# Where the operands of a split-fp32 decoder trunk start in on-chip memory: multiples of 512 bytes

## The chip, the cores and the metric

One core of a Trainium2 chip runs the whole kernel. The metric is the device time of one execution in microseconds (us). Several runs of the unchanged kernel gave a median of 1013.87 us, from 1013.25 to 1014.61.

## The reference

A two-layer causal decoder trunk on 512 tokens of width 1024, all in float32. Layer 0 mixes the tokens by a convolution module and latent attention side by side, layer 1 by causal pooling over windows of 2 to 16 tokens. After each of them stands a gated MLP with a short causal convolution on the gate branch.

```python
def conv_ffn(h, w_up, ffn_conv_w, ffn_conv_b, w_down):
    uv = h @ w_up                                  # 1024 -> 2 * 2816
    u, v = uv[..., :D_FF], uv[..., D_FF:]
    u = causal_dwconv(u, ffn_conv_w, ffn_conv_b)   # 3 taps
    return (jax.nn.silu(u) * v) @ w_down           # 2816 -> 1024

for l in range(DEPTH):                             # DEPTH = 2
    if l % 2 == 0:
        x = x + conv_mla_mixer(rmsnorm(x, norm_mix_e[e]), ...)
    else:
        x = x + pool_mixer(rmsnorm(x, norm_mix_o[o]), ...)
    x = x + conv_ffn(rmsnorm(x, norm_ffn[l]), w_up[l], ...)
return rmsnorm(x, final_norm)
```

## The kernel before

The activations lie transposed, with channels on the 128 partitions and the 512 tokens along the free dimension, so a tile of activations is 128 x 512 floats, 2048 bytes in each partition.

**Split operands.** A float32 matrix product is made of three matmuls in the type fp32r. Each operand is split into a high half (`act.copy` to fp32r, on ScalarE) and a low half (the rest, `dve.tensor_tensor` with subtract, on VectorE); `split` (L96) and `split_scaled` (L101) do that. `mm3` (L107) issues high x high (L108), high x low (L109) and low x high (L110) into one PSUM bank. Its second argument is the stationary operand (loaded into the array by a LDWEIGHTS), its third the moving one (streamed through). In nearly all stages the weights are stationary and the activations moving: 128 x 128 of weights, 512 bytes in each partition, against 128 x 512 of activations. The names in the profile follow this: `ps<-xgh,hi` is a matmul into a PSUM bank `ps` which streams the high half of an activation (`xgh`) against the high half of a weight tile (`hi`).

**Kept and streamed.** Weights are streamed: `fetch` (L147) issues a DMA of up to 128 x 1024 floats into one of three `raw` buffers, and `prepare` (L153) splits it into one of three `hi` and three `lo` buffers. All nine come from the pool "weights". One such tile serves eight stationary operands (`part`, L124), 512 bytes apart. Activations are kept: `xg` (the normed input of a stage, eight tiles and two halves, names `xgh` and `xgl`, in pools "xg0" to "xg2" on the right side of memory), `s4` (latents, attention output and convolution output, in the pool "mixer" on the left side; the profile calls them `s`), and the gate tiles (`gh` and `gl`, 22 of each, in the pool "gate", which takes the place of "mixer" later).

**Stages, in order of time.** A start in which the input and the first weights arrive and the first projection runs (to about 38 us); the other projections (to 98); keys, values and attention with convolution taps in between (to 168); the output projection (to 235); the up projection of layer 0 (22 tiles of `u` and `v`, each 24 matmuls of `mm3`'s kind) and its down projection (to 605); the pooling mixer (to 627), which first projects with the weights as moving operand (256 columns) and then multiplies by banded matrices that lie in gate tiles (L869, L870, L872); the up and the down projection of layer 1 (from 657), whose last tile runs in two halves of 256 columns (`last_down`, L751); the output. The value projection inside the attention stage (L576 to L583) swaps the roles, too: `s4` is stationary and the weights are moving, with 512 columns.

**What sets the order.** The order in which the program is written sets each engine's order; a pool's buffers set what waits for what. Neither depends on addresses.

**Where tiles start.** The pools are laid out one after the other: "consts", "resid", "weights", "temps", "small" and "mixer"/"gate" upward from the left; a pool "pad" with one tile of `PAD` floats and then "xg" downward from the right. So the size of any tile shifts all that lies behind it. Two tiles exist only to shift others: `w_pad` (L144, 128 floats ahead of `raw`) and the tile of p_pad (L273, `PAD` = 184 floats).

Of the kernel before, what the change touches and what calls it, by code (L numbers as in the profile page):

```python
# [8 lines left out]
F32 = mybir.dt.float32  # L9
# [6 lines left out]
P = 128  # L16
S = 512
# [5 lines left out]
CW = 31  # L23
# [14 lines left out]

WARM = 40
PE_TAPS = 16  # L40
PAD = 184
GLU, LAT, BLK, END = 3, 4, 2, 0


# [1 line left out]
def kernel(  # L46
# [24 lines left out]
    p_w = ctx.enter_context(tc.tile_pool(name="weights", bufs=3))  # L71
    p_t = ctx.enter_context(tc.tile_pool(name="temps", bufs=8))
# [6 lines left out]
    def uid(s):  # L79
        count[0] += 1  # L80
        return f"{s}{count[0]}"
# [7 lines left out]
    def temp():  # L89
        return p_t.tile([P, 2 + S], F32, tag="t", name=uid("t"))[:, :S]  # L90
# [25 lines left out]

    def halves(pl, tag, n, bufs):


        hl = [[pl.tile([P, S], F32R, tag=tag + i, bufs=bufs, name=uid(tag + i)) for _ in range(n)]  # L120
              for i in "hl"]
        return list(zip(*hl))
# [18 lines left out]
        stream += [(w_up[2 * NF * l + i], 1024) for i in range(2 * NF)]  # L141
        stream += [(w_down[NF * l + i], 1024) for i in range(NF)]
    raws, ready = [], []
    p_w.tile([P, P], F32, tag="pad", bufs=1, name="w_pad")  # L144
    given = [0]

    def fetch():  # L147
# [25 lines left out]

    idle = p_c.tile([P, P], mybir.dt.bfloat16, name="idle")
    dve.memset(idle, 0.0)
    misc = p_s.tile([P, 24], F32, tag="misc", bufs=1, name="misc")
    spare, floor, q_scale = misc[:, 0:1], misc[:, 4:8], misc[:, 8:12]
    mv = misc[:, 12:20].rearrange("p (a b) -> p a b", b=2)
# [91 lines left out]


    p_pad = tc.alloc_tile_pool(name="pad", bufs=1, side="right")
    p_pad.tile([P, PAD], F32, name="pad")  # L273
    p_m = tc.alloc_tile_pool(name="mixer", bufs=1, side="left", reuse_waits="tile")
    p_xg = tc.alloc_tile_pool(name="xg0", bufs=KD, side="right", reuse_waits="tile")

    def xg_tiles(pl):
        return halves(pl, "xg", KD, KD)
# [94 lines left out]
    u, ys, work, pe_work = [], [], [], []  # L373

    def conv(m):
        cw = C_CW + CW * m
        side = p_m.tile([P, S], F32, tag="side", bufs=4, name=uid("side"))
        ys.append(side)
        st = {}

        def open_acc():
            st["acc"] = aux("conv")
            act.activation(  # L383
                st["acc"], u[m][:, CW - 1 : CW - 1 + S], AF.Identity,
                bias=c(C_CB + m), scale=c(cw + CW - 1),
            )

        def pe_tap(j):
            if j == 0:
                st["acc"] = aux()  # L390
            d = p_m.tile([P, P], F32, tag="tapped", bufs=4, name=uid("tap"))
            pool.tensor_scalar(d, ident, c(cw + j), None, op0=ALU.mult)
            pe.matmul(st["acc"], d, u[m][:, j : j + S], start=j == 0, stop=j == PE_TAPS - 1)  # L393

        def tap(j):
            while m == 3 and pe_work:
                pe_work.pop(0)()
            if not st:
                open_acc()
            i = dve.scalar_tensor_tensor(  # L400
                st["acc"], u[m][:, j : j + S], c(cw + j), st["acc"],
                op0=ALU.mult, op1=ALU.add,
            )
            if held:
                tc.add_manual_dep(
                    i.ins, held.pop().ins.name,
                    mybir.DependencyInfo(
                        mybir.DependencyClass.NoSync, mybir.DependencyReason.DATA
                    ),
                    reason="background",  # L410
                )

        def close():
            bias = c(C_CB + m) if m == 3 else 0.0
            act.activation(side, st["acc"], AF.Identity, bias=bias, scale=1.0)

        n_pe = PE_TAPS if m == 3 else 0
        pe_work.extend((lambda j=j: pe_tap(j)) for j in range(n_pe))
        work.extend((lambda j=j: tap(j)) for j in range(n_pe, CW if m == 3 else CW - 1))
        work.append(close)  # L420
# [8 lines left out]
    def glu(ps_a, ps_g):  # L429
        t = temp()  # L430
        dve.tensor_tensor(t, ps_g, rows0, op=ALU.mult)
        s = temp()
        act.activation(s, t, AF.Sigmoid)
        if len(u) == 3:
            act.activation(spare, s[:, 0:1], AF.Exp)
        dve.tensor_tensor(s, s, rows0, op=ALU.mult)
        ut = p_m.tile([P, CW - 1 + S], F32, tag="u", bufs=4, name=uid("u"))
        pool.memset(ut[:, : CW - 1], 0.0)
        dve.tensor_tensor(ut[:, CW - 1 :], ps_a, s, op=ALU.mult)
        u.append(ut)  # L440
        conv(len(u) - 1)

    def s4():
        return p_m.tile([P, 2, S], F32R, tag="s4", bufs=8, name=uid("s4"))

    glu(acc4[0], acc4[1])
    glu(acc4[2], acc4[3])
    def latent(n, gain, width):
        parts, stat = [], Squares(width, dve)
# [18 lines left out]
    for _ in range(2):  # L468
        ps_a = project()
        pump(GLU)  # L470
        ps_g = project()
        glu(ps_a, ps_g)
        pump(GLU)
# [213 lines left out]
    def gslots(n):  # L687
        return halves(p_g, "g", n, NF)
# [312 lines left out]
```

## Time and profile before

| what | value |
|---|---|
| median of the runs | 1013.87 us |
| the profiled execution's own time | 1013.5 us |
| its span, from the first to the last instruction | 1011.7 us |
| instructions | 11545 |
| TensorE busy | 994.0 us, 98% of the span |
| VectorE busy | 591.6 us, 58% |
| ScalarE busy | 400.7 us, 40% |
| GpSimd busy | 70.8 us, 7% |
| DMA queue of the weights, share of 16 engines | 27.3% |
| mean granted TensorE clock | 0.995 |

PE is TensorE's matmul, PEld its weight load, DVE VectorE, ACT ScalarE, POOL GpSimd, SP the engine that issues the weight transfers. A row of instructions gives line, engine, operation, the tile written and those read, shape and type, the count, and after the bar the busy time in us and the mean ns of one; behind the second bar stands the idle time just before them and what ended it. In a table by stage, each engine has its busy us and, in parentheses, how many of its instructions touch the stage. In a view of the time line, the first two columns are the start and the length in us. Matmuls overlap each other: one record may be longer than the distance to the next start.

### The profile page before, as it was taken

Reading aid. Unit: us, or ns where it says so; the run is one execution under the profiler, and the core shown is the slowest. Engines: PE = TensorE matmul, PEld = TensorE weight load, DVE = VectorE, ACT = ScalarE, POOL = GpSimd, SP = SyncE. Lnnn points to the kernel's source line nnn. Section 1 sums busy time; section 2 is a strip of 40 time slices with the busy share of each in tenths; the row PEclk is TensorE's granted clock in tenths of the full one; section 3 lists DMA queues with packets and bytes.
Section 4 is the critical chain, followed back from the end, with each engine's and each line's share of the span. In section 5 each row is a group of like instructions: output and inputs, shape, how many; then the busy total and the mean of one; then the engine's idle time right before and its main releaser. Section 6 shows DMA issues by size and latency. Waiting matters only on the chain.

```text
span 1011.7 us, 11545 instructions
## 1 busy us (share of the span) xinstructions
PE 994.0 (98%) x4476; PEld 797.1 (79%) x4476; DVE 591.6 (58%) x915; ACT 400.7 (40%) x581; POOL 70.8 (7%) x107
## 2 busy tenths in 40 slices
PE   8999999999999999999999999999999999999996
PEld 6787676777888888888888889888888888888886
DVE  5889989856766565656332338485656555522223
ACT  6534687553433333333222236253333333332321
POOL 6000100012000000000001103100000000000101
PEclk9999999999999999999999999999999999999998
DMA  6422101113232323232222241322232223222212
GB/s 213 153 79 88 54 10 63 42 42 124 68 121 84 104 87 102 84 103 90 98 93 95 95 144 43 105 86 102 83 105 91 97 86 102 95 93 96 92 42 84
DMA packets 29478, 91.99 MB, mean 91 GB/s; under 512 B 4080, under 2 KB 6384, under 8 KB 29424
## 3 DMA queue, kind: packets, MB, share of 16 engines
q1 hardware_dynamic: 28880, 90.74, 27.3%
q8 instruction: 35, 0.57, 0.2%
q10 hardware_dynamic: 544, 0.52, 0.1%
q14 instruction: 19, 0.16, 0.0%
HBM read 89.02 MB, written 2.23 MB: 90 GB/s over the span
## 4 chain that ended last, share of the span: by engine, by line
PE 92%; DVE 4%; issue 1%; ACT 1%; DMA 0%; POOL 0%; SPq 0%; DVEq 0%
PE ps L108 28%; PE ps L110 28%; PE ps L109 28%; PE ps L558 2%; PE ps L511 1%; DVE lo L98 1%; PE aux L393 1%; PE ps L546 1%; PE aux L261 1%; PE aux L239 1%; DVE xgl L103 1%; DMA x<-in_xT_dram 0%; POOL sqr L226 0%; PE ps L869 0%; PE ps L870 0%
## 5 line engine op out<-in xcount | busy, mean ns | idle before, releaser
L108 PE MATMUL ps<-xgh,hi 128*128 128x512 f32 x816 | 324.0, 397 | 3.1 <-ACT hi L97 3.1
L97 ACT CAST hi<-raw 128x1024 fp32r<-128x1024 f32 (+2 forms) x166 | 170.0, 1026 | 394.2 <-PE ps L109 371.3
L110 PE MATMUL ps<-xgh,lo 128*128 128x512 f32 x816 | 323.3, 397 | 0.8 <-DVE lo L98 0.8
L109 PE MATMUL ps<-xgl,hi 128*128 128x512 f32 x816 | 323.4, 396 | 0.0
L98 DVE TENSOR_TENSOR lo<-raw,hi 128x1024 fp32r<-128x1024 f32 (+2 forms) x166 | 201.7, 1216 | 159.8 <-ACT hi L97 159.4
L108 PEld LDWEIGHTS ps<-xgh,hi 128*128 128x128 f32 x816 | 153.7, 188 | 40.2 <-ACT hi L97 3.7
L110 PEld LDWEIGHTS ps<-xgh,lo 128*128 128x128 f32 x816 | 153.8, 189 | 39.0 <-DVE lo L98 2.2
L109 PEld LDWEIGHTS ps<-xgl,hi 128*128 128x128 f32 x816 | 153.7, 188 | 36.6
L108 PE MATMUL ps<-gh,hi 128*128 128x512 f32 (+1 forms) x374 | 143.0, 382 | 0.0
L109 PE MATMUL ps<-gl,hi 128*128 128x512 f32 (+1 forms) x374 | 142.8, 382 | 0.0
L110 PE MATMUL ps<-gh,lo 128*128 128x512 f32 (+1 forms) x374 | 142.8, 382 | 0.0
L108 PEld LDWEIGHTS ps<-gh,hi 128*128 128x128 f32 x374 | 70.3, 188 | 15.0
L110 PEld LDWEIGHTS ps<-gh,lo 128*128 128x128 f32 x374 | 70.3, 188 | 15.0
L109 PEld LDWEIGHTS ps<-gl,hi 128*128 128x128 f32 x374 | 70.3, 188 | 15.0
L698 DVE TENSOR_TENSOR t<-ps,rows 128x512 f32<-128x512 f32 x44 | 30.4, 690 | 82.7 <-PE ps L110 82.7
L710 DVE TENSOR_TENSOR t<-ps,rows 128x512 f32<-128x512 f32 x44 | 30.4, 690 | 74.0 <-PE ps L110 74.0
L226 POOL TENSOR_TENSOR sqr<-sqr,sqr 128x512 f32<-128x512 f32 x33 | 50.5, 1529 | 322.2 <-ACT sqr L224 292.0
L400 DVE SCALAR_TENSOR_TENSOR conv<-u,col,conv 128x512 f32<-128x512 f32 x90 | 67.5, 750 | 1.6 <-ACT conv L383 0.7
L705 DVE SCALAR_TENSOR_TENSOR t<-t,col,t 128x512 f32<-128x512 f32 x88 | 65.6, 748 | 1.4
L708 ACT ACTIVATE t<-t 128x512 f32<-128x512 f32 x44 | 27.8, 632 | 74.2 <-DVE t L705 74.2
L103 DVE SCALAR_TENSOR_TENSOR xgl<-x,col,xgh 128x512 fp32r<-128x512 f32 x32 | 32.7, 1038 | 12.9 <-ACT xgh L102 12.9
L108 PE MATMUL ps<-s,hi 128*128 128x512 f32 x96 | 39.3, 421 | 0.0
(182 smaller groups left out, 813.6 us busy)
## 6 DMA issues: line engine op xcount, KB each, us to landing
raw<-in_w_up_dram SPq DMA_DIRECT2D x88, 512.0 KB, 3.3
raw<-in_w_down_dram SPq DMA_DIRECT2D x44, 512.0 KB, 3.3
raw<-in_w_in_dram SPq DMA_DIRECT2D x10, 512.0 KB, 3.3
raw<-in_w_out_dram SPq DMA_DIRECT2D x8, 512.0 KB, 3.3
x<-in_xT_dram SPq DMA_DIRECT2D x8, 256.0 KB, 4.7
raw<-in_w_in_dram SPq DMA_DIRECT2D x8, 256.0 KB, 4.0
raw<-in_w_uq_dram SPq DMA_DIRECT2D x4, 384.0 KB, 3.0
raw<-in_w_ukv_dram SPq DMA_DIRECT2D x2, 512.0 KB, 3.5
```

Of the source, the lines that this page charges most:

```text
L97: i = act.copy(dst[0], src)
L98: dve.tensor_tensor(dst[1], src, dst[0].bitcast(F32), op=ALU.subtract)
L103: dve.scalar_tensor_tensor(dst[1], src, scale, dst[0].bitcast(F32), op0=ALU.mult, op1=ALU.subtract)
L108: pe.matmul(ps, a[0], b[0], start=start, stop=False)
L109: pe.matmul(ps, a[0], b[1], start=False, stop=False)
L110: pe.matmul(ps, a[1], b[0], start=False, stop=stop)
L226: self.engine.tensor_tensor(self.parts[0], self.parts[0], t, op=ALU.add)
L400: i = dve.scalar_tensor_tensor(st["acc"], u[m][:, j : j + S], c(cw + j), st["acc"], op0=ALU.mult, op1=ALU.add,)
L698: dve.tensor_tensor(ut[:, 2 : 2 + S], pu, rows, op=ALU.mult)
L705: dve.scalar_tensor_tensor(a, ut[:, j : j + S], c(fw + j * NF + f), a, op0=ALU.mult, op1=ALU.add)
L708: act.activation(a, a, AF.Silu)
L710: dve.tensor_tensor(b, pv, rows, op=ALU.mult)
```

## The change

Three paddings replace two. `w_pad` shrinks from 128 to 48 floats, a new `t_pad` of 16 floats stands at the head of the pool "temps", and the tile of p_pad on the right shrinks from 184 to 120 floats. The tiles `u` of the convolution (542 floats used) are allocated with 640 floats, so that the tiles behind them in the pool "mixer" start on a multiple of 512 bytes too.

```diff
-PAD = 184
+W_PAD, T_PAD, R_PAD = 48, 16, 120
...
-    p_w.tile([P, P], F32, tag="pad", bufs=1, name="w_pad")
+    p_w.tile([P, W_PAD], F32, tag="pad", bufs=1, name="w_pad")
...
+    p_t.tile([P, T_PAD], F32, tag="pad", bufs=1, name="t_pad")
...
-    p_pad.tile([P, PAD], F32, name="pad")
+    p_pad.tile([P, R_PAD], F32, name="pad")
...
-        ut = p_m.tile([P, CW - 1 + S], F32, tag="u", bufs=4, name=uid("u"))
+        ut = p_m.tile([P, 640], F32, tag="u", bufs=4, name=uid("u"))[:, : CW - 1 + S]
```

The built programs have the same instructions in the same order on every engine, with the same waits, the same semaphores and the same PSUM banks. What differs is where tiles start in a partition. The bytes past a multiple of 512, by the addresses in the two built programs:

| tiles | first address before | past 512 | first address after | past 512 |
|---|---|---|---|---|
| `raw` (landing of the weights) | 38720 | 320 | 38400 | 0 |
| `hi`, `lo` (weight halves) | 51008, 63296 | 320 | 50688, 62976 | 0 |
| `xgh`, `xgl` | 195840, 212224 | 256 | 196096, 212480 | 0 |
| `s4` | 141056 | 256 | 142336 | 0 |
| `gh`, `gl` | 105728, 150784 | 256 | 105472, 150528 | 0 |
| `q`, `keys`, `v`, `prob`, `pt`, `side`, `tap` (plain fp32) | 118016 and others | 256 | 117760 and others | 0 |
| `u` (four tiles) | 124160 | 256, 384, 0, 128 | 123904 | 0 |
| temps `t` (eight tiles, 2080 bytes apart) | 76128 | 352, 384, 416, 448, 480, 0, 32, 64 | 75872 | 96, 128, and on to 320 |
| `x` (residual), `causal`, `sq` | 21824, 19776, 18240 | 320 | unchanged | 320 |

## The prediction

> **What bounds the kernel now.** I read the page first: its busy shares, then the chain that ended last, then the groups of instructions.
>
> ```profile
> span 1011.7 us, 11545 instructions
> PE 994.0 (98%) x4476; PEld 797.1 (79%) x4476; DVE 591.6 (58%) x915; ACT 400.7 (40%) x581; POOL 70.8 (7%) x107
> ...
> PE ps L108 28%; PE ps L110 28%; PE ps L109 28%; PE ps L558 2%; PE ps L511 1%; DVE lo L98 1%; PE aux L393 1%; PE ps L546 1%; PE aux L261 1%; PE aux L239 1%; DVE xgl L103 1%; DMA x<-in_xT_dram 0%; POOL sqr L226 0%; PE ps L869 0%; PE ps L870 0%
> ```
>
> TensorE is busy for 98% of the span, and 84% of the chain is the three lines of `mm3`. So the time is the number of these matmuls times the distance from one start to the next, and little else. The table by stage says the same: in the two long feed-forward stages TensorE has no idle time, at the full granted clock, while VectorE and ScalarE are far from full.
>
> ```profile
> core 0: us, PE busy (x) PEld busy (x) DVE busy (x) ACT busy (x) POOL busy (x), PEclk, DMA share, GB/s
> 0.00:38.00 38.00, 32.26 (x159) 25.82 (x160) 27.27 (x64) 20.86 (x33) 15.96 (x21) 0.96 0.63 200
> ...
> 264.00:605.00 341.00, 341.00 (x1463) 274.77 (x1462) 172.95 (x209) 118.85 (x147) 10.28 (x26) 1.00 0.30 98
> ...
> 657.00:983.00 326.00, 326.00 (x1400) 262.67 (x1399) 162.58 (x197) 113.25 (x137) 8.74 (x24) 1.00 0.27 91
> 983.00:1011.70 28.70, 19.48 (x158) 18.70 (x156) 11.42 (x40) 4.81 (x9) 4.16 (x5) 0.87 0.21 74
> ```
>
> How many are they? The groups kept apart by shape give the 512-column ones (the lines L109 and L110 of `s` are like L108's).
>
> ```profile
> L108 PE MATMUL ps<-xgh,hi 128*128 128x512 f32 x816 | 324.0, 397 | 3.1 <-ACT hi L97 3.1
> L108 PE MATMUL ps<-gh,hi 128*128 128x512 f32 x330 | 130.5, 396 | 0.0
> L108 PE MATMUL ps<-s,hi 128*128 128x512 f32 x96 | 39.3, 421 | 0.0
> ```
>
> Three matmuls for each: 3 x (816 + 330 + 96) = 3726. The recorded 396 ns is not the price, because matmuls overlap. The price is the distance between starts, and it needs a long stretch: below are the first and last starts of 300 us, and the count of the window.
>
> ```profile
> 299.66 0.39 PE L109 MATMUL ps<-xgl,hi 128*128 128x512 f32 x1
> ...
> 599.95 0.40 PE L109 MATMUL ps<-gl,hi 128*128 128x512 f32 x1
> 300.00:600.00 300.00, 300.00 (x1288) 241.70 (x1287) 143.43 (x170) 100.67 (x124) 9.78 (x21) 1.00 0.30 97
> ```
>
> 1288 records touch the window, so 1287 steps took 599.95 - 299.66 = 300.29 us: 233.3 ns a step. 3726 x 0.2333 = 869 us, 86% of the span. One nanosecond on this step is 3.7 us. This is the only term by which a change of addresses can move the total far.
>
> **The change part by part.** The built program has the same instructions on every engine, in the same order, with the same waits and semaphores; PSUM addresses are the same too. Only SBUF addresses move, so there is no new wait, and nobody queues behind anything new. Before, every weight half starts at 320 past a multiple of 512 bytes (64 past one of 256), and every activation half (`xg`, `s4`, gate) at 256. Afterwards all start at 0.
>
> *The step of the main matmuls (3726).* While one matmul streams its activations, the weights of the next are loaded, and both read SBUF:
>
> ```profile
> 400.22 0.40 PE L108 MATMUL ps<-xgh,hi 128*128 128x512 f32 x1
> 400.22 0.19 PEld L109 LDWEIGHTS ps<-xgl,hi 128*128 128x128 f32 x1
> ```
>
> Does the step depend on where the two start? The stream above moves through weight slices 512 bytes apart and through `xg` and gate tiles 2048 apart, and its mean stays at 233.3 ns from 300 to 600 us. So multiples of 512 do not matter; a dependence could only sit in the lower bits, which is what the change sets to zero. These bits differ in just three other places. In the value projection the roles are swapped, with weights (64 past a multiple of 256) streamed and `s4` (a multiple of 256) loaded:
>
> ```profile
> 102.46 0.39 PE L110 MATMUL ps<-hi,s 128*128 128x512 f32 x1
> ...
> 106.58 0.39 PE L110 MATMUL ps<-hi,s 128*128 128x512 f32 x1
> ```
>
> 18 steps in 4.12 us: 229 ns, 4.4 less. With 256 columns there are the pooling projection (weights streamed, `xg` loaded), the bands (both operands in gate tiles, both on a multiple of 256), and the last output tile (gate streamed, weights loaded), which runs at two paces:
>
> ```profile
> 606.03 0.28 PE L108 MATMUL ps<-hi,xgh 128*128 128x256 f32 x1
> ...
> 608.50 0.28 PE L108 MATMUL ps<-hi,xgh 128*128 128x256 f32 x1
> 620.09 0.28 PE L869 MATMUL ps<-gh,gh 128*128 128x256 f32 x1
> ...
> 621.29 0.28 PE L870 MATMUL ps<-gl,gl 128*128 128x256 f32 x1
> 988.33 0.28 PE L108 MATMUL ps<-gh,hi 128*128 128x256 f32 x1
> ...
> 991.39 0.28 PE L108 MATMUL ps<-gh,hi 128*128 128x256 f32 x1
> 993.75 0.28 PE L108 MATMUL ps<-gh,hi 128*128 128x256 f32 x1
> ...
> 994.81 0.28 PE L108 MATMUL ps<-gh,hi 128*128 128x256 f32 x1
> ```
>
> Counting three steps from one L108 to the next, these are 2.47 us for 21 steps (117.6 ns), 1.20 us for 10 (120.0), 3.06 us for 27 (113.3), and 1.06 us for 9 (117.8). The last two have the same kinds of address, so part of such differences is a phase that the stream falls into after an interruption, not the address. That is why I don't read the 4.4 ns of the value projection as the price of alignment, but as a bound.
>
> The bounds for the step after the change, then. Below: 229 ns, or, if two half-width steps of 113.3 make a whole one, 226.7 ns; that is 4.4 to 6.7 ns less, 16 to 25 us. Above: the only place where both operands already stand on a multiple of 256, as all will, is the bands, and it is the slowest of the half-width ones, by 120.0 - 117.7 = 2.3 ns or 120.0 - 113.3 = 6.7 ns; 9 to 25 us more. I take 233.3, no change, because it is the nearest row in shape and roles, it held in every stage with this layout, and the rows that differ point in both directions.
>
> The Trainium skill bears on this twice. The Trainium skill, "TensorE: Matmul & The Clock Gate", Part 2, says that the PE reads the streamed and the loaded operand through two independent SBUF ports, so that loading weights steals nothing from the running matmul; by that rule no start address matters and the sum is no change. Its spacing of N/2.4 + 2.5 ns (same part, "Back-to-back issue gap") would be 216 ns here, though, and the trace shows 233, so by this formula something does take 17 ns and no run here yet says what. The Trainium skill, "SBUF — State Buffer", Specifications, gives 16 bytes as the line that an access should stay in; all operands were on multiples of 64 already, so by it too nothing changes.
>
> *The half-width steps of the other places.* The last output tile has 3 x 44 = 132, the pooling projection 96. If all went to the bands' 120 ns: at most 228 x 6.7 ns = 1.5 us more; if all to 113.3, 0.4 us less for the 96. Taken at 0; it lies inside the range.
>
> *Plain fp32 matmuls* (scores, values, taps). The taps stream from starts 4 bytes apart, and the recorded times don't differ from those of scores and values on multiples of 256:
>
> ```profile
> L393 PE MATMUL aux<-u,tap 128*128 128x512 f32 x32 | 16.3, 592 | 0.0
> L511 PE MATMUL ps<-keys,q 128*128 128x512 f32 x16 | 8.2, 592 | 0.0
> ```
>
> So 0. *VectorE and ScalarE.* The eight temps stand at eight different places within 512 bytes, and the 90 taps start 4 bytes apart, yet the spread is a few ns:
>
> ```profile
> L698 DVE TENSOR_TENSOR t<-ps,rows x44: 679/692/693, 264.8 to 870.0; 128x512 f32<-128x512 f32 x44
> L400 DVE SCALAR_TENSOR_TENSOR conv<-u,col,conv x90: 735/750/758, 44.4 to 177.9; 128x512 f32<-128x512 f32 x90
> ```
>
> So 0, and even 2% would be hidden: VectorE works 173 us of 341 in the long stage. *Transfers.* The weights land on another offset. Outside the start they are hidden (DMA 30% busy). In the first 38 us, where TensorE lacks 38.00 - 32.26 = 5.7 us, the 256 KB transfers take
>
> ```profile
> x<-in_xT_dram SPq DMA_DIRECT2D x8, 256.0 KB, 4.7
> raw<-in_w_in_dram SPq DMA_DIRECT2D x8, 256.0 KB, 4.0
> ```
>
> and a few per cent of 4 us is 0.2 us either way; taken at 0.
>
> Sum: 0 against the profiled execution's own 1013.5 us (span 1011.7 and 1.8 around it), which is 0.4 below the median of the runs, 1013.87. Forecast: 1013.9 us. What a measurement of this kernel can tell from no change is about 0.2%, 2 us, or 0.5 ns of the step.
>
> **The rivals.**
>
> *A shorter step.* Mechanism: the stream and the weight load get in each other's way at some relative offset, and 64 bytes of offset cost something that 0 does not. For it: 229 ns in the value projection, 113.3 in part of the last tile. Against it: the bands, at offset 0, have neither. Price: 229 to 226.7 ns, 989 to 997 us. If the step were shorter, VectorE's 173 of 341 us in the long stage would still be short of full, so nothing else would come to be the limit.
>
> *A much shorter step.* Mechanism: the whole excess over an undisturbed stream goes. A plain fp32 matmul's record is 592 ns, and its tail should be that of the others, 396 - 233 = 163; it steps at 429 ns, for two passes, so a pass takes 214.5. Price: 18.8 ns x 3726 = 70 us, 944 us; anything from there to 985 counts here. Against it: no row with fp32r operands comes near. The 216 ns of the Trainium skill's page on TensorE would lead there too.
>
> *A longer step (the other side).* Mechanism: with both operands at the same place within 512 bytes, stream and load start on the same part of the memory at the same moment, and one waits. For it: the bands, in the same relation, are the slowest, and their weight loads are the only steadily longer ones, 192 ns against 188:
>
> ```profile
> L869 PEld LDWEIGHTS ps<-gh,gh 128*128 128x128 f32 x20 | 3.8, 192 | 0.0
> ```
>
> Against it: one wait at the start may vanish in a 512-column stream. Price: 2.3 to 6.7 ns, 1022 to 1039 us; it decides from 0.5 ns a step on.
>
> **How the numbers follow.** No change 0.33; shorter step 0.25; much shorter 0.12; longer 0.30. Faster by over 0.2% is the second and third, 0.37; same 0.33; slower 0.30. The likeliest single case is no change, 1013.9 us, with 1012 to 1016 as its own range. The range for 8 in 10 leaves out the much shorter step and a tail of the longer: 985 to 1040 us.
>
> **What would show it.** The count of matmuls will be equal, and all else is read from two starts far apart in a long stage: 233.3 ns a step if I am right, 227 to 229 or 236 to 240 for the rivals, with the time following at 3.7 us per ns. The bands should stay at 120.0, since their two operands keep their relation. I am wrong if the step moves by more than 0.5 ns, or if the time moves while the step does not, which would point to the start or to a stage in which TensorE waits.

## The result: 2.2% faster, through the step of the main matmuls

The changed kernel takes 991.95 us (median of five runs, 990.70 to 993.05) against 1013.87 us (1012.57 to 1014.61 in these runs). The ratio is 0.9782, with a 95% interval from 0.9771 to 0.9793. The forecast of no change was wrong; what came is the rival "a shorter step", with the shortest step that it named, 226.7 ns.

The page of the changed kernel, its busy shares and its chain:

```profile
span 990.5 us, 11545 instructions
PE 973.5 (98%) x4476; PEld 799.1 (81%) x4476; DVE 591.3 (60%) x915; ACT 400.6 (40%) x581; POOL 70.7 (7%) x107
...
PE ps L108 28%; PE ps L109 28%; PE ps L110 28%; PE ps L558 2%; PE ps L511 2%; DVE lo L98 1%; PE aux L393 1%; PE ps L546 1%; PE aux L261 1%; PE aux L239 1%; DMA x<-in_xT_dram 0%; DVE xgl L103 0%; DMA col<-in_cols_dram 0%; PE ps L870 0%; PE ps L869 0%
```

The number of instructions is the same, the shares are within two percentage points, and the bound is the same: TensorE is busy 98% of the time, and 84% of the chain is the three lines of `mm3`. Only the span is 21.2 us shorter. The two starts of the time line that are far apart, and the count of the window between them, say why:

```profile
299.64 0.39 PE L108 MATMUL ps<-xgh,hi 128*128 128x512 f32 x1
...
590.00 0.39 PE L108 MATMUL ps<-gh,hi 128*128 128x512 f32 x1
300.00:590.00 290.00, 290.00 (x1282) 240.11 (x1280) 143.08 (x169) 100.29 (x123) 9.75 (x21) 1.00 0.31 100
```

1281 steps in 290.36 us are 226.7 ns a step, where the kernel before had 233.3. The granted clock is 1.00 in both, so it is not a clock that differs. The stages by their own windows (the same stages as before, shifted by what was saved ahead of them; the columns are those of the table by stage in the prediction):

```profile
0.00:38.00 38.00, 33.05 (x162) 27.20 (x163) 27.27 (x64) 20.90 (x34) 15.93 (x21) 0.96 0.64 201
...
264.00:592.00 328.00, 328.00 (x1448) 271.60 (x1448) 170.72 (x206) 117.45 (x146) 10.24 (x26) 1.00 0.31 101
...
644.80:961.00 316.20, 316.20 (x1396) 261.81 (x1395) 162.25 (x196) 113.00 (x137) 8.76 (x24) 1.00 0.29 94
961.50:990.50 29.00, 19.80 (x157) 19.06 (x155) 11.26 (x40) 4.81 (x9) 4.15 (x5) 0.87 0.21 73
```

By the starts in the two traces, the place where the time was saved is:

| stretch | before | after | saved |
|---|---|---|---|
| up to the uninterrupted feed-forward stretch of layer 0 | 264.0 us | 261.8 us | 2.2 us |
| that stretch, 1462 steps | 341.3 us | 331.6 us | 9.7 us |
| pooling mixer, to the same stretch of layer 1 | 52.0 us | 51.4 us | 0.6 us |
| that stretch, 1396 steps | 325.9 us | 316.7 us | 9.2 us |
| last tile (half-width) and output | 28.5 us | 29.0 us | -0.5 us |

Nearly all of it lies in the two uninterrupted stretches, at 6.6 ns for each of 2858 steps. The full 3726 steps at 6.6 ns would be 24.6 us. Of the missing 3.4 us, 1.8 are in the 744 steps of the main kind before 264 us, which saved 3.1 us and not 4.9, and another 0.9 us went back into the other work of those 264 us. Some 1.2 us of these 2.7 are the clock and not the step. For 3.4 us of this profile the granted clock was 0.50, where the kernel before had 1.00 (the row of the changed kernel first, then that of the kernel before at the same place):

```profile
201.10:204.40 3.30, 3.30 (x13) 2.91 (x13) 1.29 (x2) 3.30 (x7) 0.10 (x1) 0.50 0.48 159
203.30:206.70 3.40, 3.35 (x17) 2.64 (x18) 1.29 (x2) 3.40 (x6) 0.10 (x1) 1.00 0.45 154
```

From the second group of four `L648` matmuls to the first L109 behind them it is 2.21 us before (203.34 to 205.55) and 3.43 us here (200.93 to 204.36). The sixth kernel below, which has the same distances, has 1.00 there. A further part is settling: the stream is interrupted often before 264 us, and after an interruption the step needs some matmuls until it is steady. The start of the long stretch shows it in the time line. Its first six steps take 263.14 - 261.76 = 1.38 us, 230 ns each, before it runs at 226.7 for good:

```profile
261.76 0.39 PE L109 MATMUL ps<-xgl,hi 128*128 128x512 f32 x1
261.99 0.40 PE L110 MATMUL ps<-xgh,lo 128*128 128x512 f32 x1
262.23 0.39 PE L108 MATMUL ps<-xgh,hi 128*128 128x512 f32 x1
262.45 0.40 PE L109 MATMUL ps<-xgl,hi 128*128 128x512 f32 x1
262.69 0.39 PE L110 MATMUL ps<-xgh,lo 128*128 128x512 f32 x1
262.92 0.39 PE L108 MATMUL ps<-xgh,hi 128*128 128x512 f32 x1
263.14 0.39 PE L109 MATMUL ps<-xgl,hi 128*128 128x512 f32 x1
```

A last 0.5 us went back into the last tile.

### The profile page after: what moved, and what is told of

Same layout as the page of the kernel before. It is cut to its first block, busy times and chain, and to the rows that moved or that the text cites. A ratio compares the mean times of both kernels' runs of the same rounds, so it can differ in the third digit from the quotient of the medians.

```text
span 990.5 us, 11545 instructions
## 1 busy us (share of the span) xinstructions
PE 973.5 (98%) x4476; PEld 799.1 (81%) x4476; DVE 591.3 (60%) x915; ACT 400.6 (40%) x581; POOL 70.7 (7%) x107
## 4 chain that ended last, share of the span: by engine, by line
PE 93%; DVE 4%; DMA 1%; issue 1%; SPq 0%; ACT 0%; DVEq 0%
PE ps L108 28%; PE ps L109 28%; PE ps L110 28%; PE ps L558 2%; PE ps L511 2%; DVE lo L98 1%; PE aux L393 1%; PE ps L546 1%; PE aux L261 1%; PE aux L239 1%; DMA x<-in_xT_dram 0%; DVE xgl L103 0%; DMA col<-in_cols_dram 0%; PE ps L870 0%; PE ps L869 0%
## 5 line engine op out<-in xcount | busy, mean ns | idle before, releaser
L108 PE MATMUL ps<-xgh,hi 128*128 128x512 f32 x816 | 319.3, 391 | 2.0 <-ACT hi L97 1.8
L110 PE MATMUL ps<-xgh,lo 128*128 128x512 f32 x816 | 318.0, 390 | 0.8 <-DVE lo L98 0.8
L109 PE MATMUL ps<-xgl,hi 128*128 128x512 f32 x816 | 318.4, 390 | 0.0
L109 PEld LDWEIGHTS ps<-xgl,hi 128*128 128x128 f32 x816 | 153.7, 188 | 31.8
L109 PE MATMUL ps<-gl,hi 128*128 128x512 f32 (+1 forms) x374 | 140.9, 377 | 0.0
L110 PE MATMUL ps<-gh,lo 128*128 128x512 f32 (+1 forms) x374 | 140.8, 376 | 0.0
L109 PEld LDWEIGHTS ps<-gl,hi 128*128 128x128 f32 x374 | 70.4, 188 | 12.7
```

Source lines behind the costliest of these rows:

```text
L108: pe.matmul(ps, a[0], b[0], start=start, stop=False)
L109: pe.matmul(ps, a[0], b[1], start=False, stop=False)
L110: pe.matmul(ps, a[1], b[0], start=False, stop=stop)
```

## The experiments

Twelve kernels, in which only paddings, tile sizes or the size of weight loads differ. Where nothing else is said, the edit is made on the changed kernel. What they test is a distance. I write d for the place where the loaded operand starts minus the place where the streamed one starts, in bytes, modulo 256. In the kernel before, the feed-forward stages load weights at 320 past a multiple of 512 and stream activations at 256: d = 64. The changed kernel has d = 0 everywhere. Theory R says that d sets the step. Theory A says that an operand's own start does (on a multiple of 512, or, in its weaker form A128, of 128). For each kernel I show the table by stage for 270 to 460 us (the up projection: weights against `xg`) and 490 to 590 us (the down projection: weights against gate tiles). A record is 0.39 us long, so 1.7 of the records counted in a window reach over its edge; the steps are the count less 1.7. For the kernels before and after these rows are, in this order,

```profile
270.00:460.00 190.00, 190.00 (x816) 153.07 (x815) 113.76 (x144) 72.95 (x92) 1.89 (x19) 1.00 0.29 94
490.00:590.00 100.00, 100.00 (x430) 80.55 (x430) 30.06 (x31) 26.14 (x30) 7.00 (x5) 1.00 0.28 95
```

```profile
270.00:460.00 190.00, 190.00 (x840) 157.34 (x839) 117.19 (x148) 73.64 (x91) 1.88 (x19) 1.00 0.30 97
490.00:590.00 100.00, 100.00 (x443) 82.77 (x442) 33.70 (x34) 30.92 (x39) 8.26 (x6) 1.00 0.33 106
```

so 816 and 430 matmuls mean 233.3 ns, and 840 and 443 mean 226.7. The steps given below are the same count made on single starts.

**1. Only the weights move, by 64 bytes (d = 0, no operand on a multiple of 512).** Edit on the kernel before:

```diff
-    p_w.tile([P, P], F32, tag="pad", bufs=1, name="w_pad")
+    p_w.tile([P, 112], F32, tag="pad", bufs=1, name="w_pad")
...
+    p_t.tile([P, 16], F32, tag="pad", bufs=1, name="t_pad")
```

> The kernel before with the weights alone moved back by 64 bytes, so that weights and activations all start 256 past a multiple of 512. Theory R (only the distance between the streamed and the loaded operand, modulo 512, matters): the distance becomes 0, the step of the 512-column matmuls falls from 233.3 to 226.7 ns and the time to 992 us, all of the gain. Theory A (each operand must itself start on a multiple of 512): nothing is on a multiple of 512, the step stays at 233 and the time at 1014 us. Theory A128 (the weights alone were at fault, being only on a multiple of 64): 226.7, as R.

```profile
270.00:460.00 190.00, 190.00 (x840) 157.43 (x839) 117.20 (x148) 73.75 (x91) 1.88 (x19) 1.00 0.30 97
490.00:590.00 100.00, 100.00 (x443) 82.86 (x442) 33.33 (x34) 30.95 (x39) 8.26 (x6) 1.00 0.34 106
```

992.43 us against 1014.27, ratio 0.9782 (0.9766 to 0.9799), the step 226.7 ns in both stages. All of the gain comes with the 64 bytes of the weights, and with every operand at 256 past a multiple of 512. Multiples of 512 play no part.

**2. Weights and `xg` at 64, gate tiles at 0 (d = 0 up, 64 down).** Edit on the changed kernel:

```diff
-W_PAD, T_PAD, R_PAD = 48, 16, 120
+W_PAD, T_PAD, R_PAD = 64, 128, 104
```

> The changed kernel with weights at 64, xg at 64 and gate tiles at 0 past a multiple of 512. Theory R: the up projection (distance 0) keeps 226.7 ns although both operands are on multiples of 64 only; the down projection (distance 64, as before) goes back to 233.3. Theories A and A128: weights off 128, so both stages go to 229 to 233 ns.

```profile
270.00:460.00 190.00, 190.00 (x840) 157.34 (x839) 117.14 (x148) 74.44 (x94) 1.99 (x20) 1.00 0.30 97
490.00:590.00 100.00, 100.00 (x430) 80.17 (x429) 32.50 (x34) 29.06 (x36) 8.26 (x6) 1.00 0.31 98
```

One run, 1000.72 us. One kernel has both paces: 226.7 ns where both operands stand at 64, and 233.3 ns where the same weights meet gate tiles at 0. That is R; A in either form would have had the first stage slow.

**3. Weights at 0, `xg` at 64, gate tiles at 256 (d = -64 up, 0 modulo 256 down).** W_PAD, T_PAD, R_PAD = 48, 80, 104.

> The changed kernel with weights at 0, xg at 64, gate tiles at 256. Theory R: up projection at distance -64, as the value projection before: 229 ns; down projection at distance 256, not seen so far: no number, anything from 226 to 234. Theory A: both stages 229 to 233, since the streamed operand is off a multiple of 512. Theory A128: up 229 to 233, down 226.7.

```profile
270.00:460.00 190.00, 190.00 (x832) 156.04 (x831) 115.51 (x145) 72.50 (x90) 1.88 (x19) 1.00 0.30 97
490.00:590.00 100.00, 100.00 (x443) 82.83 (x442) 33.49 (x34) 30.25 (x38) 8.26 (x6) 1.00 0.33 105
```

One run, 996.00 us. A distance of 256 counts as none: 226.7 ns. A distance of -64 gives 228.9 ns, which is what the value projection had in the kernel before, where the streamed weights stood 64 past a multiple of 256 and the loaded `s4` on one (18 steps in 4.12 us).

**4. Weights at 128, `xg` at 64, gate tiles at 0 (d = 64 up, 128 down).** W_PAD, T_PAD, R_PAD = 80, 112, 104.

> The changed kernel with weights at 128, xg at 64, gate tiles at 0. Theory R: up projection at distance 64: 233.3 ns; down projection at distance 128: not seen so far, no number. Theory A: both 229 to 233. Theory A128: up 229 to 233 (xg off 128), down 226.7.

```profile
270.00:460.00 190.00, 190.00 (x816) 152.39 (x815) 113.77 (x144) 72.74 (x91) 1.89 (x19) 1.00 0.29 94
490.00:590.00 100.00, 100.00 (x432) 81.13 (x431) 30.91 (x31) 26.15 (x31) 6.99 (x5) 1.00 0.30 95
```

One run, 1012.61 us: 233.3 ns at 64, and an irregular 232.4 ns at 128 (single steps from 227 to 242). A128 had expected 226.7 there.

**5. Distances of 32 (d = -32 up, 32 down).** W_PAD, T_PAD, R_PAD = 48, 72, 112.

> The changed kernel with weights at 0, xg at 32, gate tiles at 224 past a multiple of 256 (distance of the loaded from the streamed operand: -32 in the up projection, +32 in the down projection, modulo 256). If the step depends on the distance in whole units of 64 bytes, -32 gives 226.7 or 229 ns and +32 gives 226.7 or 233.3. If it depends on the distance smoothly, something between these. A still shorter step, under 226, would show that distance 0 is not the best.

```profile
270.00:460.00 190.00, 190.00 (x816) 152.82 (x815) 114.03 (x144) 72.90 (x91) 1.89 (x19) 1.00 0.29 94
490.00:590.00 100.00, 100.00 (x430) 80.63 (x429) 30.05 (x31) 26.08 (x30) 7.00 (x5) 1.00 0.29 95
```

One run, 1014.53 us: 233.3 ns on both sides. That the distance might count in units of 64 is gone, and -32 is worse than -64.

**6. A distance of 16, missed.** W_PAD, T_PAD, R_PAD = 48, 76, 116.

> As the run with 32 bytes, but xg at 16 and gate tiles at 240: distances -16 and +16. In units of 64 bytes: the same steps as at -32 and +32. Smooth: nearer to 226.7 than these.

```profile
270.00:460.00 190.00, 190.00 (x840) 157.30 (x840) 117.17 (x147) 73.30 (x90) 1.88 (x19) 1.00 0.30 97
490.00:590.00 100.00, 100.00 (x443) 82.81 (x442) 33.56 (x34) 30.10 (x38) 8.26 (x6) 1.00 0.33 108
```

One run, 991.45 us, 226.7 ns in both stages. But the built program starts tiles on multiples of 32 bytes and rounded the 16 away: `xg` stood at 0 and the gate tiles at 256. It repeats d = 0 and tests nothing of 16; the last experiment makes up for it.

**7. Distances of 96 and 160 (d = 96 up, 160 down).** W_PAD, T_PAD, R_PAD = 48, 40, 80.

> As before it, with xg at 160 and gate tiles at 96: distances +96 (up projection) and +160 (down projection), modulo 256. Units of 64 bytes: up 233.3 or 232.4 as at 64 and 128, down 232.4 or 229.1 as at 128 and 192. Smooth: up 232.9, down 231.

```profile
270.00:460.00 190.00, 190.00 (x813) 152.74 (x812) 114.73 (x145) 72.91 (x91) 1.89 (x19) 1.00 0.29 93
490.00:590.00 100.00, 100.00 (x431) 80.43 (x430) 30.88 (x30) 25.68 (x30) 7.01 (x5) 1.00 0.30 95
```

One run, 1017.00 us: 234.3 and 233.3 ns, where neither theory of the expectation had more than 233.3 for the first. So a padding can also be worse than the one before. The value projection of this kernel loads `s4` from 96 and streams weights from 0, so its distance is 96 too, with the roles swapped; its 18 steps from 103.23 to 107.45 us take 234.4 ns each.

**8. The changed kernel with half of one load in three.** What the load costs was the next question: with L one assumes that the step falls as the load gets shorter, with F that 226.7 ns is a floor for another reason.

```diff
-        pe.matmul(ps, a[0], b[1], start=False, stop=False)
+        pe.matmul(ps[0:64], a[0][:, 0:64], b[1], start=False, stop=False)
```

> The changed kernel in which the second matmul of each triple (high x low) loads only 64 of its 128 weight columns; the upper 64 output rows lack this product. Theory L (what a step has above an undisturbed pass of 214.5 ns comes from the weight load that runs beside it): the step from L108 to L109, beside which the short load runs, falls by half of its excess, from 226.7 to about 220 ns, the others stay. Theory F (the excess is a fixed cost of changing weights or of the pass): all three stay at 226.7, and the long stretches at 680 ns for three.

```profile
270.00:460.00 190.00, 190.00 (x828) 140.44 (x827) 116.64 (x147) 74.16 (x93) 1.99 (x20) 1.00 0.29 95
```

and among its groups of weight loads the halved one:

```profile
L109 PEld LDWEIGHTS ps<-xgl,hi 128*64 128x64 f32 x816 | 109.9, 135 | 34.4
```

One run, 1003.16 us. The load is shorter, 135 ns, where the changed kernel has 188, and the step is longer, 229.8 ns. Both L and F are wrong.

**9. The activations on multiples of 512, the weights left at 320 (d = 64).** W_PAD, T_PAD, R_PAD = 128, 64, 120 in the changed kernel: the other half of the change alone.

> The changed kernel with the weights alone put back to 320 past a multiple of 512; all activations stay on multiples of 512. Theory R (distance modulo 256): the distance is 64 everywhere, so the step is 233.3 ns and the time that of the kernel before, 1014 us, although xg, s4 and gate tiles have all that the change gave them. Theory A (each operand that is put on a multiple of 512 gives its share): a step between 226.7 and 233.3 and a time between 992 and 1014 us.

```profile
270.00:460.00 190.00, 190.00 (x816) 152.29 (x815) 113.75 (x143) 72.75 (x91) 1.89 (x19) 1.00 0.30 94
490.00:590.00 100.00, 100.00 (x430) 80.17 (x429) 30.55 (x30) 26.01 (x30) 6.97 (x5) 1.00 0.30 95
```

1013.11 us against 1014.25, ratio 0.9991 (0.9981 to 1.0000), the step 233.3 ns. All activations, the plain fp32 tiles and the convolution's `u` are where the change puts them, and 0.1% comes of it, 0.2% at most by the interval.

**10 and 11. Half of nearly every load, at d = 0 and at d = 64.** The same edit on the changed kernel and on the kernel before:

```diff
-        pe.matmul(ps, a[0], b[0], start=start, stop=False)
-        pe.matmul(ps, a[0], b[1], start=False, stop=False)
-        pe.matmul(ps, a[1], b[0], start=False, stop=stop)
+        m, e = P if start else 64, P if stop else 64
+        pe.matmul(ps[0:m], a[0][:, 0:m], b[0], start=start, stop=False)
+        pe.matmul(ps[0:64], a[0][:, 0:64], b[1], start=False, stop=False)
+        pe.matmul(ps[0:e], a[1][:, 0:e], b[0], start=False, stop=stop)
```

> The changed kernel with only 64 weight columns in all matmuls of a triple except the first and the last of each accumulation; the upper 64 output rows lack those products. Theory L (the excess over an undisturbed pass of 214.5 ns comes from the weight load beside it): the step falls, to about 220 ns. Theory F (the excess belongs to the pass or to the change of weights): about 227 ns. The run with one short load in three gave neither, but 229.8; if this one is above 226.7 too, a shorter load is no cheaper, and what counts is how the two run against each other.

> The same edit on the kernel before. Theory L: from 233.3 to about 224 ns. Theory F: 233.3. If the distance of the operands matters only while both are read, halving the load halves what distance 64 costs over distance 0.

The up projection of the two, on the changed kernel and on the kernel before:

```profile
270.00:460.00 190.00, 190.00 (x828) 114.51 (x827) 116.40 (x147) 73.53 (x92) 2.01 (x20) 1.00 0.29 95
```

```profile
270.00:460.00 190.00, 190.00 (x817) 113.90 (x816) 114.22 (x145) 73.22 (x92) 1.89 (x19) 1.00 0.29 94
```

One run each, 1002.14 and 1012.34 us. At d = 0 the step is 229.8 to 230.0 ns, in a pattern of six steps from 224 to 236 ns; at d = 64 it is 232.75 ns. Neither goes below 226.7, although the loads take 134 ns now. That the time of the load is what the step waits for is not so. With half the load the distance of 64 costs 2.9 ns where it cost 6.7, near the half that the last expectation named, but mostly because the step at d = 0 got longer by 3.2 ns; the one at d = 64 got shorter by 0.6. The edit also lets these matmuls write only 64 rows of PSUM, and no run separates that from the shorter load. So a part of the load in the cost is argued, not shown.

**12. A distance of 16, made inside the tile (d = -16 up, 0 down).** `xg` tiles of 576 floats, of which the floats 4 to 515 are used; two temps less make room.

```diff
-W_PAD, T_PAD, R_PAD = 48, 16, 120
+W_PAD, T_PAD, R_PAD = 48, 32, 120
...
-        return halves(pl, "xg", KD, KD)
+        hl = [[pl.tile([P, S + 64], F32R, tag="xg" + i, bufs=KD, name=uid("xg" + i))[:, 4 : 4 + S]
+               for _ in range(KD)] for i in "hl"]
+        return list(zip(*hl))
```

> The changed kernel with six temps in place of eight and xg tiles of 576 floats, of which floats 4 to 515 are used: xg starts 16 past a multiple of 256, weights and gate tiles on one. Up projection at distance -16: if the step depends on units of 32 bytes, 226.7 or 233.3; if of 16 bytes, another number, and one under 226 would be a better place than that of the change. The down projection at distance 0 stays at 226.7.

```profile
270.00:460.00 190.00, 190.00 (x822) 154.22 (x821) 115.09 (x146) 73.38 (x92) 1.91 (x19) 1.00 0.29 94
490.00:590.00 100.00, 100.00 (x443) 82.81 (x442) 33.44 (x34) 28.51 (x34) 7.07 (x6) 1.00 0.31 99
```

One run, 1005.68 us: 231.7 ns at -16, 226.7 at 0 in the same kernel. Zero is a narrow optimum.

The whole curve, for 512 columns of fp32r:

| d modulo 256 | step | where |
|---|---|---|
| 0 | 226.7 ns | the changed kernel, 1, 2 (up), 3 (down), 6, 12 (down) |
| -16 | 231.7 ns | 12 (up) |
| 32, -32 | 233.3 ns | 5 |
| 64 | 233.3 ns | the kernel before, 2 (down), 4 (up), 9 |
| -64 | 228.9 ns | 3 (up); the value projection of the kernel before |
| 96 | 234.3 ns | 7 (up; value projection) |
| 128 | 232.4 ns | 4 (down) |
| 160 | 233.3 ns | 7 (down) |

No version that beats the changed kernel was found; the first experiment equals it within the spread of the runs with one padding made smaller and one added.

## Why the prediction was wrong

**What bounds the kernel: right.** The count of 3726, the step as the only large term and its price of 3.7 us per ns held. 6.6 ns less give 24.6 us by that price, 21.2 came; most of the rest is accounted for above.

**The step after the change: wrong, and this is the step that failed.** The prediction took 233.3 ns "because it is the nearest row in shape and roles, it held in every stage with this layout, and the rows that differ point in both directions". But the row's layout, d = 64, was the very thing that the change took away, so that it held everywhere said nothing about d = 0. The rows that differed were the evidence, and two readings of them were wrong:

- The 229 ns of the value projection were taken "as a bound", not as the price of alignment, because the half-width steps of the last tile showed two paces with the same kinds of address. The third experiment made the same distance in another stage, with the roles the other way round, and got the same 228.9 ns over some 800 steps. It was the price of its distance. The 18 steps alone could not have told, though. In the changed kernel, at d = 0, the same 18 take the same 4.12 us:

```profile
100.43 0.40 PE L110 MATMUL ps<-hi,s 128*128 128x512 f32 x1
...
102.51 0.39 PE L110 MATMUL ps<-hi,s 128*128 128x512 f32 x1
...
104.55 0.39 PE L110 MATMUL ps<-hi,s 128*128 128x512 f32 x1
```

The first nine of them still settle (2.08 us, 231 ns each), and only the last nine run at 226.7 (2.04 us). The doubt about a phase after an interruption was right for a stretch this short; what was wrong was to take no change from it.

- The bands, at d = 0, were read as a sign for a longer step at 512 columns. As a reading of half-width steps that was right: with the change the other half-width places went to the bands' pace. But for 512 columns the order is reversed: no distance gave a clearly longer step than d = 0 with 256 columns, and none a shorter one with 512. Half-width rows bound nothing at full width here. Nor were the bands the only place with both operands on a multiple of 256: the scores and values were such a place too, though in plain fp32.

The rows of the changed kernel for that, the pooling projection and the bands:

```profile
595.91 0.28 PE L108 MATMUL ps<-hi,xgh 128*128 128x256 f32 x1
...
597.11 0.28 PE L109 MATMUL ps<-lo,xgh 128*128 128x256 f32 x1
606.69 0.28 PE L869 MATMUL ps<-gh,gh 128*128 128x256 f32 x1
...
607.89 0.28 PE L870 MATMUL ps<-gh,gl 128*128 128x256 f32 x1
```

Ten steps in 1.20 us are 120.0 ns, in the projection (117.6 before) and in the bands (120.0 before). "The bands should stay at 120.0" was right, and for the reason given, since their two operands keep their relation. The second sign that spoke for a longer step, the bands' weight loads of 192 ns, belongs to 256 columns as well. The loads of the pooling projection went from 188 to 192 ns when its distance became 0, while those beside 512 columns stayed at 188:

```profile
L108 PEld LDWEIGHTS ps<-hi,xgh 128*128 128x128 f32 x28 | 5.4, 192 | 0.0
```

**The rival's number: right by the wrong route.** 226.7 ns was worked out as two half-width steps of 113.3. Those belong to d = 64; at d = 0 two half-width steps are 240. That the measured step is 226.7 too is luck as far as this sum goes.

**The rival's mechanism: right as far as it went.** It spoke of a relative offset of which 64 bytes cost something that 0 does not; the first two experiments and the ninth show just that. "Multiples of 512 do not matter" and "a dependence could only sit in the lower bits" held as well: the period is 256 (third experiment). A rule had been weighed against it, the Trainium skill, "TensorE: Matmul & The Clock Gate", Part 2, by which the loaded and the streamed operand come through independent ports and loading takes nothing from the running matmul. The runs disagree with what the prediction drew from it, that no start address matters: the step moves from 226.7 to 234.3 ns with nothing but the distance between the two. Whether it is the two reads that collide, no run shows.

**Much shorter: did not come.** No distance and no shorter load that was tried brought the mean step below 226.7 ns. The 214.5 ns are an estimate, half of the 429 ns from one plain fp32 matmul of 512 columns to the next (L393). The two passes in it rest on a ratio in the trace of the kernel before: with 128 columns, plain fp32 matmuls (L546) come 108 to 109 ns apart and the last ten of bf16 (L183) 56 ns. What the remaining distance to 214.5 is made of stays open.

**The small terms: right.** The half-width steps cost some 0.5 us in the last tile and, at 2.4 ns for each of 96, 0.2 us in the pooling projection (1.5 at most was said). Plain fp32 matmuls still take 592 ns:

```profile
L393 PE MATMUL aux<-u,tap 128*128 128x512 f32 x32 | 16.3, 592 | 0.0
```

Transfers of 256 KB at the start landed in 4.4 and 3.4 us (4.7 and 4.0 before). TensorE's idle time in the first 38 us is 38.00 - 33.05 = 4.95 us, 0.8 less than before; among all kernels here it lies between 4.7 and 6.4 without relation to their paddings, so I read no gain from alignment into it. And with the shorter step nothing else became the limit: VectorE works 171 of 328 us in the long stretch of layer 0.

**What stays open.** No run shows what in the memory or in TensorE has a period of 256 bytes. Nor is it known whether the streamed operand's distance to the load of the next matmul counts, or to that of its own: all tiles of a kind have the same residue here, so no run separates the two. It also stays open why the sign of d matters (228.9 at -64, 233.3 at 64), and why a shorter load at d = 0 makes the step longer.

## What to carry to other kernels

This is one kernel, with fp32r operands of 512 and 256 columns. In another one bound by fp32r matmuls with a weight load beside each, read the start addresses of the streamed and of the loaded operand modulo 256 from the built program, and give the two the same residue: here one padding of 64 bytes was worth 2.2%, and putting everything on multiples of 512 nothing beyond it. Judge it by the distance of two starts over some hundred matmuls, in every stage, since a kernel can have several distances; and try 256-column matmuls by themselves, for here they were faster at other distances. When a forecast takes "no change" from the row nearest in shape, ask first whether that row has the property that the change removes.

## What the runs showed of the hardware that was not expected

- The step of a 512-column fp32r matmul depends on the distance of its two operands in the partition modulo 256 bytes: 226.7 ns at 0, 231.7 already at -16, 228.9 at -64, 233.3 at 32 and 64, 234.3 at 96. Which of the two is the weight and which the activation made no difference at -64 (228.9 both ways) and at 96 (234.3 and 234.4). Where the two lie for themselves makes no difference (226.7 ns with both at 0, both at 64 and both at 256).
- With 256 columns it is the other way round: 120.0 ns at distance 0, 113.3 to 117.8 at 64, 117.6 at -64, and the weight loads take 192 ns at distance 0 where they take 188 at -64.
- Weight loads of half the size (134 ns, not 188) made the step at distance 0 longer, 229.8 to 230.0 ns, and at distance 64 shorter, 232.75 ns.
- At distance 0 the step takes two to nine matmuls (224 to 236 ns) after an interruption until it runs at its 226.7 ns, so short bursts gain less than the long stretches: the 18 steps of the value projection take 4.12 us at distance -64 and at 0.
